# Layer 1's memory queries begin with their first halves, and the first two pairs' values are split in token layout

## The chip, the cores and the metric

The kernel runs on one NeuronCore of one Trainium2 chip, as one launch. The metric is the device time of a launch in microseconds (us), given as the median of several runs. A profile is one execution, recorded by the hardware profiler; its times count from the first instruction of the span.

## The reference

A two-layer decoder trunk on 1024 tokens of width 1024, in float32. Layer 0 mixes a causal multi-scale pooling branch with a cross-attention into 256 memory tokens (4 heads of 128). After it, one projection of the residual stream gives shared keys, values and forget-gate logits. Layer 1 mixes a forgetting attention (16 heads of 64) over these with another memory cross-attention. Cut to what matters here:

```python
def mixer_sublayer(x, mem, w_in, w_mem_kv, w_out, main_fn):
    h = x @ w_in                                  # columns [main | mem q | main gate | mem gate]
    ...
    y_mem = memory_attention(q_mem, mem, w_mem_kv)
    y = jnp.concatenate([y_main * silu(g_main), y_mem * silu(g_mem)], axis=-1)
    return y @ w_out

def memory_attention(q_mem, mem, w_mem_kv):
    mkv = mem @ w_mem_kv                          # keys, values of the 256 memory tokens, 4 heads of 128
    p = softmax(q @ mk.T * 128 ** -0.5)
    return p @ mv

def shared_kv(x, w_kv_shared, b_forget):
    h = x @ w_kv_shared                           # k | v | forget logits
    cum = cumsum(log_sigmoid(f_logit + b_forget), axis=1)

def forgetting_attention(u, k, v, cum):           # causal, 16 heads of 64
    logits = q @ k.T * 0.125 + cum[t] - cum[s]
    return softmax(logits) @ v

x = layer_norm(ALPHA * x + mixer_sublayer(...))   # per layer
```

## The kernel before

Everything is computed with each float32 operand split into a high part (fp32r) and a low part (bf16), three products for one (`three`: high by high, low by high, high by low). `hi_lo` makes the parts: ScalarE casts the high one (line 187), VectorE or GpSimd subtracts for the low one (line 188). A weight slab comes by `split_w`: a DMA into one of four `raw` buffers, then `hi_lo` into one of four `w` and four `wl` buffers. `slab` is one projection of 128 output columns for all 1024 tokens: two weight pieces of 256 KB, then two halves of 512 tokens, 24 products each, every half into one of the two PSUM banks `pj` and evicted from there.

TensorE runs in the order in which the program is written. The other engines and the DMA queue of SyncE run in an order that a scheduler fixes when the kernel is built; each queue is in order, so an instruction that waits holds all behind it.

At the end of layer 0 (`OutProj.rest`, `norm`) the rows of the new residual stream are normed in tiles of 128 tokens, scaled to float16, turned by two DMA transposes each (`turned_rows`) and written to `XH`, `XL`, the transposed operand of all of layer 1's projections. The last two row tiles, 6 and 7, are turned inside `mem_attention` of layer 1 (the list `turns`), before its products.

`mem_attention(1, ...)` then makes four memory keys (`keys(h)`, 24 products of 256 columns each, from `memT`, which `mem_kv` loads and splits), and after that four query slabs `win[1, 8 + h]` with the memory values (`vals(h)`) between them. Its attention over 8 row tiles follows, with gate slabs as filling.

`start_units` makes queries and keys of the first head pair and, through `v_first`, the values of the first two pairs with the forget logits, token by token. `v_turned` turns these values to channel layout with 16 transposes on TensorE and scales and splits them per channel (`values_of`), and four DMA transposes bring them back to token layout. `forget_gates` computes log-sigmoid on VectorE, sums over tokens with one product by a triangle and seven by ones, and writes the sums to DRAM (`cumd`), from which `forget_rows` loads one row per head, broadcast over the partitions (`R`). The sixteen heads of `fox` follow; each softmax needs its `R`.

In the last pair, `OutProj.early` multiplies the first 256 rows of the memory branch's output by its part of the output weights, into four accumulators: two in banks `L`, two in `pj`. The gate slabs just before use `pj` as well.

Of the kernel before, what the change touches and what calls it, by code (L numbers as in the profile page):

```python
# [77 lines left out]
def run(units):  # L78
    for _ in units:
        pass  # L80
# [19 lines left out]
def trunk_kernel(ctx, tc, x, xT, memT, win, wk, wv0, wv, wmk, wmv, wout, poolw, pscale, lng, lnb, bforget, out):  # L100
# [96 lines left out]
        nc.gpsimd.tensor_scalar(hi, src, 1.0, 1.0, ALU.mult, ALU.mult)  # L197
        nc.gpsimd.tensor_tensor(lo[0], src, hi.bitcast(F32), ALU.subtract)  # L198

    def split_w(src_dram, shape, by=nc.vector):  # L200
        r = raw(shape)
        nc.sync.dma_start(r, src_dram)
        h, l = in_place(wt, shape)
        gp_hi_lo(h, l, r) if low[0] else hi_lo(h, l, r, by=by)
        return h, l

# [21 lines left out]
        for i, (a, b) in enumerate(terms):  # L228
            nc.tensor.matmul(acc, a, b, start=i == 0, stop=i == len(terms) - 1)  # L229

    def slab(pieces_dram, XH, XL, evac, banks=("pj", 2)):

        ready = isinstance(pieces_dram, list)
        if ready:
            ws = pieces_dram
        else:
            ws = [split_w(pieces_dram[0], [P, 4, P])]
            yield 0
            ws.append(split_w(pieces_dram[1], [P, 4, P]))
            yield 0  # L240

        def terms(n, kts):
            cols = slice(n * NH, (n + 1) * NH)
            out = []
            for kt in kts:
                h, l = ws[kt // 4]
                out.append(three((h[:, kt % 4, :], cut(l, slice(None), kt % 4)), (XH[:, kt, cols], cut(XL, slice(None), kt, cols))))
            return out

        def put(acc, a, b, start, stop):  # L250
            nc.tensor.matmul(acc, a, b, start=start, stop=stop)  # L251
# [117 lines left out]

    def mem_attention(l, XH, XL, kv, qtile, ytile, yd):  # L370

        (kh, kl, v, undo), keys, vals = kv
        qs = []
        if l:
            while turns:
                turns.pop(0)(lambda: vt([P, D], F16), lambda: vt([P, 2 * KT, P], F16))
            for h in range(4):
                keys(h)
        for h in range(MH):
            qh, ql = in_place(qtile, [P, S])  # L380
# [8 lines left out]
            if not l or h:  # L389
# [62 lines left out]
    class OutProj:  # L452
# [68 lines left out]
        def early(self, y, yh, yl):  # L521


            nc.sync.dma_start(y, self.yd[2, :, :, : 2 * P])
            yield
            for two in (slice(0, 2), slice(2, 4)):
                hi_lo(yh[:, two, :], cut(yl, slice(None), two), y[:, two, :], True)
                yield
            self.accs = self.open(0)
            yield from self.products(self.accs, 2, yh, yl)  # L530

        def rest(self, resid, XH, XL, dst):
            self.split(24)
# [169 lines left out]
    with tc.tile_pool(name="in1", bufs=1) as in1:  # L703
# [7 lines left out]
        def vt(shape, dt=F32R):  # L711
            return sb(shape, "V", 4, dt, in1)

        kv = mem_kv(1)
        with tc.manual_schedule(engines={PE}):
            mem_attention(1, XH, XL, kv, xy, lambda: vt([P, S], F32), y1d[2])
        cumd = dram.tile([HEADS, S], F32, name="cumd")
        fg = G((P, 8, ST * HEADS))
        flog = fg[:, 0, :]
# [18 lines left out]
        unscale, done = const.tile([P, 8], F32, name="unscale"), []  # L738
        toks, first_vs = [], []

        def v_turned():

            for pr in range(2):
                u = MK([P, S], F32)
                for g in range(2):
                    t = ps([P, 4, P], "T", 2)
                    for j in range(4):
                        nc.tensor.transpose(t[:, j, :], toks[g][:, j, pr * P : (pr + 1) * P], ident)
                    nc.scalar.copy(u[:, g * NH : (g + 1) * NH], t.rearrange("p s q -> p (s q)"))
                    yield  # L750
                first_vs.append(values_of(u))

        def v_first():

            wh, wl = zip(*(halved(MK, [P, 4, FW]) for _ in range(2)))
            toks.extend(T([P, 4, 2 * P], F32) for _ in range(2))
            for kt in range(KT):
                r = raw([P, FW])
                nc.sync.dma_start(r, wv0[kt // 2, :, kt % 2, :])
                hi_lo(wh[kt // 4][:, kt % 4, :], cut(wl[kt // 4], slice(None), kt % 4), r)  # L760
            for s in range(ST):
                acc = ps([P, NH], "L", 3)
                terms = []
                for kt in range(KT):
                    at = slice(None), kt, slice(s * P, (s + 1) * P)
                    terms.append(three((XH[at], cut(XL, *at)), (wh[kt // 4][:, kt % 4, :], cut(wl[kt // 4], slice(None), kt % 4))))
                for j, (u, w) in enumerate(grouped(terms, s % 2 == 1)):
                    nc.tensor.matmul(acc[:, :FW], u, w, start=j == 0, stop=j == 3 * KT - 1)
                    yield FW
                nc.scalar.copy(toks[s // 4][:, s % 4, :], acc[:, : 2 * P])  # L770
                nc.vector.tensor_tensor(flog[:, s * HEADS : (s + 1) * HEADS], acc[:, 2 * P : FW], bfb, ALU.add)

        def forget_gates():

            n = ST * HEADS
            a, e, z, q, acc, lf, cum = (fg[:, j, :] for j in range(1, 8))
            lp = a
            nc.vector.tensor_scalar(a, flog, -1.0, None, ALU.mult)
            nc.vector.tensor_tensor(a, a, flog, ALU.max)
            nc.scalar.activation(e, a, AF.Exp, scale=-1.0)  # L780
            nc.vector.tensor_scalar(z, e, 2.0, None, ALU.add)
            nc.vector.reciprocal(z, z)
# [12 lines left out]
            nc.tensor.matmul(ca[:, :n], tri, lf, start=True, stop=False)  # L795
            for d in range(1, ST):
                nc.tensor.matmul(ca[:, d * HEADS : n], ones, lf[:, : n - d * HEADS], start=False, stop=d == ST - 1)
            nc.vector.tensor_copy(cum, ca[:, :n])
            yield
            t = ps([P, 4, P], "T", 2)  # L800
            nc.tensor.transpose(t[:, 0, :], cum, ident)
            rows = tr[:, 0, :]
            nc.vector.tensor_copy(rows, t[:, 0, :])
            for i in range(ST):
                nc.sync.dma_start(cumd[:, i * P : (i + 1) * P], rows[i * HEADS : (i + 1) * HEADS, :])
            yield
# [57 lines left out]
        def start_units(keys, queries, following):  # L864
# [299 lines left out]
```

## Time and profile before

| | |
|---|---|
| median of 3 runs | 1215.21 us (1212.19 to 1216.25) |
| the profiled execution | 1217.81 us, its span 1215.6 us |
| TensorE busy | 1180.0 us, 97% of the span |
| VectorE busy | 798.4 us, 66% |
| ScalarE busy | 616.6 us, 51% |
| GpSimd busy | 200.4 us, 16% |
| granted TensorE clock | 0.996 of full speed |

In rows of the profile, PE is TensorE, DVE is VectorE, ACT is ScalarE, POOL is GpSimd and SPq the DMA queue of SyncE. A timeline row gives start, duration, engine, line, operation, output<-inputs by tile names, count, and in brackets the idle time ahead of it with what ended it. A window row gives for a stretch its length and the busy time of PE, PEld (weight loads), DVE, ACT and POOL, then the granted clock, the DMA engines' share and GB/s. Where rows merge several matmuls, the recorded ends overlap; the pace is read from start to start.

### The profile page before, as it was taken

How to read it: one execution, taken by the hardware profiler on the slowest of the kernel's cores; microseconds unless marked ns; L12 is line 12 of the kernel's file. 1: busy time of each engine (PE TensorE's matmuls, PEld its weight loads, DVE VectorE, ACT ScalarE, POOL GpSimd, SP SyncE). 2: the span in 40 equal slices, each digit the busy share in tenths (PEclk: the TensorE clock that was granted, in tenths of full speed). 3: DMA queues.
4: the chain of work that ended last, by engine and by line, in shares of the span. 5: the costliest groups of instructions: out<-in, count | busy, mean ns of one | idle time of the engine just before them, and what ended most of it. 6: DMA issues, size and time to landing. Idle time of an engine off the chain costs nothing. (4 is left out here: it accounts for less than half of the span.)

```text
span 1215.6 us, 19488 instructions
## 1 busy us (share of the span) xinstructions
PE 1180.0 (97%) x6837; PEld 743.0 (61%) x6954; DVE 798.4 (66%) x1868; ACT 616.6 (51%) x1318; POOL 200.4 (16%) x304
## 2 busy tenths in 40 slices
PE   8999999999999997999999999999999999999997
PEld 4566665555555555666775666666666666655554
DVE  6644767375666657357555878777878878775654
ACT  6433654262522235356333777767766777783110
POOL 2000000000000012100003334333334324530000
PEclk9999999999999999999999999999999999999998
DMA  6333654242445567245527789889897999995431
GB/s 234 108 102 93 133 113 156 78 130 71 142 153 156 156 173 184 77 107 103 175 53 170 158 184 182 177 169 187 176 194 165 196 178 210 235 234 181 167 110 47
DMA packets 284305, 182.83 MB, mean 150 GB/s; under 512 B 229168, under 2 KB 242608, under 8 KB 284208
## 3 DMA queue, kind: packets, MB, share of 16 engines
q1 hardware_dynamic: 284208, 181.59, 61.4%
q8 instruction: 54, 0.88, 0.3%
q14 instruction: 43, 0.35, 0.1%
HBM read 94.97 MB, written 22.61 MB: 97 GB/s over the span
## 5 line engine op out<-in xcount | busy, mean ns | idle before, releaser
L251 PE MATMUL pj<-A,w 128*128 128x512 f32 (+1 forms) x1887 | 600.5, 399 | 3.6 <-ACT A L187 2.2
L251 PE MATMUL pj<-A,wl 128*128 128x512 bf16 x951 | 360.7, 381 | 4.8 <-DVE wl L188 0.6
L251 PEld LDWEIGHTS pj<-A,w 128*128 128x128 f32 x976 | 180.8, 189 | 45.7 <-ACT A L187 3.1
L251 PEld LDWEIGHTS <-w 128*128 128x128 bf16 x992 | 95.8, 98 | 123.3 <-issue 36.0
L251 PEld LDWEIGHTS <-wl 128*128 128x128 bf16 x992 | 97.5, 98 | 95.1 <-issue 5.8
L915 ACT ACTIVATE T<-MK,s 128x512 f32<-128x512 f32 x192 | 111.0, 578 | 58.0 <-DVE s L907 36.7
L937 DVE SCALAR_TENSOR_TENSOR P<-T,s,P 128x512 f16<-128x512 f32 x192 | 111.9, 613 | 31.5 <-ACT P L936 30.0
L936 ACT ACTIVATE P<-T,s 128x512 f16<-128x512 f32 x192 | 102.6, 575 | 48.7 <-issue 27.4
L518 PEld LDWEIGHTS <-T 128*128 128x128 bf16 x736 | 70.6, 98 | 87.3 <-issue 4.4
L188 DVE TENSOR_TENSOR wl<-raw,w 128x512 bf16<-128x512 f32 x98 | 69.2, 712 | 82.8 <-ACT w L187 81.4
L187 ACT CAST w<-raw 128x512 fp32r<-128x512 f32 x106 | 64.8, 617 | 98.5 <-PE pj L251 67.6
L229 PE MATMUL L<-B,B 128*128 128x512 f32 (+3 forms) x384 | 109.9, 389 | 3.2 <-DVE s L907 2.9
L229 PEld LDWEIGHTS L<-B,B 128*128 128x128 f32 x384 | 71.1, 189 | 28.5 <-DVE s L907 9.0
L351 POOL TENSOR_SCALAR A<-A 128x1024 bf16<-128x1024 f32 x8 | 8.4, 1052 | 423.5 <-ACT A L349 423.5
L907 DVE CUSTOM_DVE_ANT_0 MK<-L,R 128x512 f32<-128x512 f32 (+3 forms) x128 | 72.5, 567 | 8.4 <-DMA R<-cumd 5.0
L899 POOL TENSOR_SCALAR_AFFINE_SELECT R<-R 128x128 f32<-128x128 f32 x128 | 41.4, 329 | 207.8 <-DVE s L907 111.5
L198 POOL TENSOR_TENSOR wl<-raw,w 128x512 bf16<-128x512 f32 x54 | 69.1, 1280 | 3.5
L188 DVE TENSOR_TENSOR T<-T,T 128x1024 bf16<-128x1024 f32 x23 | 31.9, 1387 | 50.8 <-ACT T L187 50.7
L187 ACT CAST T<-T 128x1024 fp32r<-128x1024 f32 x23 | 24.1, 1048 | 76.9 <-DMA T<-y1d 50.4
L197 POOL TENSOR_SCALAR w<-raw 128x512 fp32r<-128x512 f32 x54 | 34.3, 634 | 74.8 <-PE pj L251 74.7
L518 PE MATMUL L<-B,T 128*128 128x512 bf16 (+1 forms) x164 | 43.0, 391 | 0.2
L966 PE MATMUL O<-T,V 128*128 128x128 f16 x576 | 38.5, 220 | 4.8 <-DMA T<-P 4.8
(277 smaller groups left out, 1744.1 us busy)
## 6 DMA issues: line engine op xcount, KB each, us to landing
raw<-in_win_dram SPq DMA_DIRECT2D x96, 256.0 KB, 2.9
raw<-in_wout_dram SPq DMA_DIRECT2D x40, 256.0 KB, 2.9
B<-B SPq DMA_DIRECT2D x32, 256.0 KB, 4.9
R<-cumd SPq DMA_DIRECT2D x16, 512.0 KB, 4.5
y0d<-Y SPq DMA_DIRECT2D x12, 512.0 KB, 3.2
T<-y0d SPq DMA_DIRECT2D x12, 512.0 KB, 5.3
T<-y1d SPq DMA_DIRECT2D x11, 512.0 KB, 4.2
raw<-in_wmk_dram SPq DMA_DIRECT2D x16, 256.0 KB, 2.7
```

The costliest lines, as they stand in the source:

```text
L187: pin(nc.scalar.copy(hi, src))
L188: pin(by.tensor_tensor(lo[0], src, hi.bitcast(F32), ALU.subtract))
L198: nc.gpsimd.tensor_tensor(lo[0], src, hi.bitcast(F32), ALU.subtract)
L229: nc.tensor.matmul(acc, a, b, start=i == 0, stop=i == len(terms) - 1)
L251: nc.tensor.matmul(acc, a, b, start=start, stop=stop)
L518: nc.tensor.matmul(acc, y, w, start=c == 2 and j == firsts[id(acc)], stop=c == 1 and j == lasts[id(acc)])
L899: nc.gpsimd.affine_select(R[:, qs], R[:, qs], [[-1, P]], ALU.is_ge, -NEG, base=0, channel_multiplier=1).ins
L907: nc.vector.tensor_tensor_reduce(p[:, lo:up], lg, R[:, lo:up], 1.0, top, ALU.add, ALU.min, m[:, n : n + 1])
L915: nc.scalar.activation(e, p[:, lo:up], AF.Exp, bias=top, scale=-1.0, accum_out=sums[:, n, hd % 2, i : i + 1],)
L936: nc.scalar.activation(pair[:, lo:up], e, AF.Copy, scale=r)
L937: nc.vector.scalar_tensor_tensor(pair[:, L + lo : L + up], e, r, pair[:, lo:up], ALU.mult, ALU.subtract)
L966: nc.tensor.matmul(acc[:, cols(i)], v[:, b, 2 * j : 2 * j + 2, :].rearrange("p e d -> p (e d)"), pt[hd, i][:, j, :], start=n == 0, stop=Fa ...
```

## The change

There are three edits. In layer 1's `mem_attention` the order becomes: weights of all four query slabs, the first two on the `w` and `wl` buffers, the last two on buffers of the pool `P` (`aside_homes`); the turns of row tiles 6 and 7; the first halves (tokens 0 to 511) of all four queries; only then `mem_kv` with its loads of `memT`; then each query's second half with keys and values between and behind. In `start_units`, `v_split` takes the place of `v_turned`: one scale for all values of the first two pairs (a maximum over both tiles, across partitions by one transpose, spread again by one product with ones), and the split straight into token layout, without the 16 transposes and the four DMA transposes. The gates' tile sums are made by six additions on VectorE, so that one product with ones stands where seven stood. And `OutProj.early` multiplies first for the accumulators in `L` and then for those in `pj`.

```diff
-    def slab(pieces_dram, XH, XL, evac, banks=("pj", 2)):
+    def slab(pieces_dram, XH, XL, evac, banks=("pj", 2), make=wt):
...
     def mem_attention(l, XH, XL, kv, qtile, ytile, yd):
 
-        (kh, kl, v, undo), keys, vals = kv
-        qs = []
+        qs = [in_place(qtile, [P, S]) for _ in range(MH)] if l else []
+
+        def query_units(h, make):
+            qh, ql = qs[h]
+            return slab(win[l, 8 + h], XH, XL, lambda cols, acc: hi_lo(qh[:, cols], cut(ql, slice(None), cols), acc), make=make)
+
+        def aside_homes():
+
+            lows = sb([P, 4, 4, P], "P", 4, BF16)
+            for n in range(2):
+                highs = sb([P, 2, 4, P], "P", 4, F32R)
+                left = [[highs[:, k], lows[:, 2 * n + k]] for k in range(2)]
+                yield lambda shape, dt=F32R, left=left: left[0].pop(0) if dt == F32R else left.pop(0)[0]
+
         if l:
+            homes = aside_homes()
+            units = [query_units(h, wt if h < 2 else next(homes)) for h in range(MH)]
+            for two in units:
+                run(islice(two, 2))
             while turns:
                 turns.pop(0)(lambda: vt([P, D], F16), lambda: vt([P, 2 * KT, P], F16))
-            for h in range(4):
-                keys(h)
-        for h in range(MH):
-            qh, ql = in_place(qtile, [P, S])
-            units = slab(win[l, 8 + h], XH, XL, lambda cols, acc: hi_lo(qh[:, cols], cut(ql, slice(None), cols), acc))
-            if l and not h:
-                run(islice(units, 3 * KT + 2))
-                vals(0)
-            run(units)
-            qs.append((qh, ql))
-            if not l:
+            for two in units:
+                run(islice(two, 3 * KT))
+            kv = mem_kv(l)
+        (kh, kl, v, undo), keys, vals = kv
+        for h in range(MH):
+            if l:
+                run(units[h])
+                for what, which in ((), ((keys, 0), (keys, 1)), ((keys, 2), (vals, 0)), ((keys, 3), (vals, 1)))[h]:
+                    what(which)
+            else:
...
+        if l:
+            vals(2)
+            vals(3)
...
-            yield from self.products(self.accs, 2, yh, yl)
+            parts = self.terms(self.accs, 2, yh, yl)
+            yield from self.ordered(grouped(parts[0] + parts[1]) + grouped(parts[2] + parts[3], True), 2)
...
-        def v_turned():
+        def v_split():
+
+            m, e = tiny(2), tiny(1)
+            for g in range(2):
+                nc.vector.tensor_reduce(
+                    m[:, g : g + 1], toks[g].rearrange("p s t -> p (s t)"), AX.X, ALU.max, apply_absolute_value=True,
+                )
+            nc.vector.tensor_tensor(e, m[:, 0:1], m[:, 1:2], ALU.max)
+            yield
+            row, all_ = ps([P, NH], "L", 3), ps([P, NH], "L", 3)
+            nc.tensor.transpose(row[:1, :P], e, ident)
...
+            nc.tensor.matmul(all_[:, :1], ones[:1, :], top[:1], start=True, stop=True)
...
+                for b in range(2):
+                    u, (hi, lo) = toks[pr][:, :, 64 * b : 64 * b + 64], (v[:, b, e::2, :] for e in range(2))
+                    nc.scalar.activation(hi, u, AF.Copy, scale=sc)
+                    nc.vector.scalar_tensor_tensor(lo, u, sc, hi, ALU.mult, ALU.subtract)
...
+            nc.vector.tensor_copy(q[:, :HEADS], lf[:, :HEADS])
+            for d in range(1, ST - 1):
+                own, before = (slice((d - k) * HEADS, (d - k + 1) * HEADS) for k in range(2))
+                nc.vector.tensor_tensor(q[:, own], q[:, before], lf[:, own], ALU.add)
+
             yield
             ca = ps([P, 2 * P], "O", 1)
             nc.tensor.matmul(ca[:, :n], tri, lf, start=True, stop=False)
-            for d in range(1, ST):
-                nc.tensor.matmul(ca[:, d * HEADS : n], ones, lf[:, : n - d * HEADS], start=False, stop=d == ST - 1)
+            nc.tensor.matmul(ca[:, HEADS:n], ones, q[:, : n - HEADS], start=False, stop=True)
...
             gates = forget_gates()
             next(gates)
-            for _ in v_turned():
-                yield from islice(own, 6)
-            yield from islice(own, 33)
+            split = v_split()
+            yield from islice(own, 45)
+            next(split)
+            yield from islice(own, 31)
             next(gates)
             yield from islice(own, 7)
             next(gates)
+            for n in (8, 14):
+                yield from islice(own, n)
+                next(split)
             yield from own
```

ScalarE's queue at the seam of the layers, before. `raw..` are loaded pieces, `w..` query or key weights, `MK..<-pj..` evictions of memory keys; `V663` and `V666` are the scaled rows of tiles 6 and 7, `A500<-V..` their way into `XH`.

```order
L344 ACTIVATE V663_4081<-G636_3998,unrow_3145 128x1024
L187 CAST w685_4184<-raw684_4182 128x512
L580 ACTIVATE s647_4029<-s646_4028 128x1
L187 CAST MK658_4074<-pj669_4101 128x256
L187 CAST w688_4190<-raw687_4188 128x512
L194 CAST MK659_4075<-MK658_4074 128x256
L349 ACTIVATE A500_3059<-V665_4085,unrow_3145 128x8x128
```

The same place after the change. `T687` and `T689` are the two halves of `memT`, `P660` the fourth query's weights, `B650<-pj683` and `B652<-pj684` the evictions of the first halves of queries 0 and 1; `V677` and `V680` are row tiles 6 and 7.

```order
L344 ACTIVATE V677_4103<-G636_3998,unrow_3145 128x1024
L187 CAST T687_4231<-raw691_4235 128x512
L194 CAST T688_4232<-T687_4231 128x512
L187 CAST T687_4231<-raw692_4240 128x512
L194 CAST T688_4232<-T687_4231 128x512
L349 ACTIVATE A500_3059<-V679_4107,unrow_3145 128x8x128
L600 ACTIVATE s647_4029<-s646_4028 128x1
L187 CAST P660_4062<-raw675_4095 128x512
L187 CAST P660_4062<-raw676_4099 128x512
L187 CAST B650_4052<-pj683_4123 128x512
L187 CAST T689_4233<-raw693_4245 128x512
L187 CAST T689_4233<-raw694_4250 128x512
```

The rows right behind these:

```order
L194 CAST T690_4234<-T689_4233 128x512 x2
L344 ACTIVATE V680_4113<-G643_4020,unrow_3145 128x1024
L187 CAST B652_4054<-pj684_4150 128x512
L349 ACTIVATE A500_3059<-V682_4117,unrow_3145 128x8x128
L187 CAST B654_4056<-pj685_4177 128x512
```

What moved: the casts of `memT`, which stood ahead of row tile 6, now stand around it, and the query evictions stand among the turns of tiles 6 and 7, each behind a load.

SyncE's queue at the seam, before. `raw..` are the four buffers in turn, `x1` the store of row tile 6, `V665` that tile's turned rows.

```order
L289 DMA raw656_4064<-in_memT_dram 128x512
L289 DMA raw657_4069<-in_memT_dram 128x512
L202 DMA raw670_4102<-in_wmk_dram 128x512
L202 DMA raw673_4108<-in_wmk_dram 128x512
L202 DMA raw677_4142<-in_wmk_dram 128x512
L202 DMA raw680_4148<-in_wmk_dram 128x512
L202 DMA raw684_4182<-in_wmk_dram 128x512
L589 DMA x1_177<-G636_3998 128x1024
L202 DMA raw687_4188<-in_wmk_dram 128x512
L202 DMA raw691_4222<-in_wmk_dram 128x512
L202 DMA raw694_4228<-in_wmk_dram 128x512
L347 DMA_TRANSPOSE V665_4085<-V663_4081 128x8x128
```

The same place after the change; `V679` is the turned tile 6.

```order
L202 DMA raw673_4087<-in_win_dram 128x512
L202 DMA raw674_4091<-in_win_dram 128x512
L609 DMA x1_177<-G636_3998 128x1024
L202 DMA raw675_4095<-in_win_dram 128x512
L202 DMA raw676_4099<-in_win_dram 128x512
L289 DMA raw691_4235<-in_memT_dram 128x512
L289 DMA raw692_4240<-in_memT_dram 128x512
L347 DMA_TRANSPOSE V679_4107<-V677_4103 128x8x128
L348 DMA_TRANSPOSE V679_4107<-V678_4104 128x8x128
L289 DMA raw693_4245<-in_memT_dram 128x512
L289 DMA raw694_4250<-in_memT_dram 128x512
```

What moved: the query weights have the buffers first, and the two halves of `memT` stand on both sides of tile 6's transposes.

The DMA queue of SyncE between the gates and the first head, before. `cumd` are the gates' sums, `R` the rows of the first two heads, `V..<-MK..` the values' DMA transposes, `raw1030`, `raw1049` and `raw1052` weight loads.

```order
L735 DMA_TRANSPOSE V954_5943<-MK950_5931 128x16x64 x2
L822 DMA B914_5574<-B913_5573 64x1024 x2
L822 DMA B916_5576<-B915_5575 64x1024 x2
L735 DMA_TRANSPOSE V962_5991<-MK958_5979 128x16x64 x2
L202 DMA raw1030_6311<-in_win_dram 128x512
L805 DMA cumd_5551<-G906_5553 16x128 x8
L202 DMA raw1049_6382<-in_win_dram 128x512
L202 DMA raw1052_6392<-in_win_dram 128x512
L884 DMA R981_6153<-cumd_5551 128x1024
```

After the change:

```order
L865 DMA B909_5569<-B908_5568 64x1024 x2
L865 DMA B911_5571<-B910_5570 64x1024 x2
L202 DMA raw1017_6286<-in_win_dram 128x512
L202 DMA raw1036_6357<-in_win_dram 128x512
L202 DMA raw1039_6367<-in_win_dram 128x512
L848 DMA cumd_5546<-G901_5548 16x128 x8
L931 DMA R968_6128<-cumd_5546 128x1024
```

What moved: the four transposes are gone, and two weight loads stand ahead of the sums that stood behind them.

More of the change, by code (lines that the diff above doesn't have):

```diff
@@ L236, in slab @@
         else:
-            ws = [split_w(pieces_dram[0], [P, 4, P])]
+            ws = [split_w(pieces_dram[0], [P, 4, P], make=make)]
             yield 0
-            ws.append(split_w(pieces_dram[1], [P, 4, P]))
+            ws.append(split_w(pieces_dram[1], [P, 4, P], make=make))
             yield 0
@@ L712, in vt @@
             return sb(shape, "V", 4, dt, in1)
-        kv = mem_kv(1)
         with tc.manual_schedule(engines={PE}):
-            mem_attention(1, XH, XL, kv, xy, lambda: vt([P, S], F32), y1d[2])
+            mem_attention(1, XH, XL, None, xy, lambda: vt([P, S], F32), y1d[2])
         cumd = dram.tile([HEADS, S], F32, name="cumd")
@@ L739, in trunk_kernel @@
         toks, first_vs = [], []
-        def v_turned():
-            for pr in range(2):
[L744 to L751, printed above, removed]
+        def v_split():
[8 more added lines that the diff above has]
+            nc.tensor.transpose(row[:1, :P], e, ident)
+            top = tiny(1)
+            nc.vector.tensor_reduce(top[:1], row[:1, :P], AX.X, ALU.max)
+            nc.vector.tensor_scalar(top[:1], top[:1], 2.0 ** -100, None, ALU.max)
+            nc.vector.tensor_scalar(top[:1].bitcast(I32), top[:1].bitcast(I32), 0x7F800000, None, ALU.bitwise_and)
+            yield
+            nc.tensor.matmul(all_[:, :1], ones[:1, :], top[:1], start=True, stop=True)
+            un, sc = unscale[:, :1], tiny(1)
+            nc.vector.tensor_scalar(un, all_[:, :1], 2.0 ** -15 / PSCALE, None, ALU.mult)
+            nc.vector.reciprocal(sc, all_[:, :1])
+            nc.vector.tensor_scalar(sc, sc, 2.0 ** 14, None, ALU.mult)
+            for pr in range(2):
+                done.append(0)
+                v = vt([P, 2, 2 * ST, 64], F16)
+                for b in range(2):
+                    u, (hi, lo) = toks[pr][:, :, 64 * b : 64 * b + 64], (v[:, b, e::2, :] for e in range(2))
+                    nc.scalar.activation(hi, u, AF.Copy, scale=sc)
+                    nc.vector.scalar_tensor_tensor(lo, u, sc, hi, ALU.mult, ALU.subtract)
+                first_vs.append((v, un))
+            yield
@@ L753, in v_first @@
         def v_first():
             wh, wl = zip(*(halved(MK, [P, 4, FW]) for _ in range(2)))
-            toks.extend(T([P, 4, 2 * P], F32) for _ in range(2))
+            toks.extend(T([P, ST, P], F32) for _ in range(2))
             for kt in range(KT):
@@ L769, in v_first @@
                     yield FW
-                nc.scalar.copy(toks[s // 4][:, s % 4, :], acc[:, : 2 * P])
+                for pr in range(2):
+                    nc.scalar.copy(toks[pr][:, s, :], acc[:, pr * P : (pr + 1) * P])
                 nc.vector.tensor_tensor(flog[:, s * HEADS : (s + 1) * HEADS], acc[:, 2 * P : FW], bfb, ALU.add)
```

7 lines of the change are left out of this document (4 added, 3 removed).

## The prediction

> **What bounds the kernel now.** I read the page first, then the busy time by stretches, then TensorE's waits in the stretches that the edits touch, then the timelines of the engines that it waits for there.
>
> ```profile
> span 1215.6 us, 19488 instructions
> PE 1180.0 (97%) x6837; PEld 743.0 (61%) x6954; DVE 798.4 (66%) x1868; ACT 616.6 (51%) x1318; POOL 200.4 (16%) x304
> 456.00:482.80 26.80, 20.60 (x147) 15.36 (x147) 20.33 (x32) 15.18 (x29) 8.94 (x6) 1.00 0.79 193
> PE pj L229 <- DVE T L188: 2.8, 1, 2.8
> ```
>
> TensorE bounds the kernel: 97% busy, 35.6 us idle in all. So only two things can pay: products that go away, and waits that go away and don't come back. The second stretch of interest is the seam of the layers, 456.0 to 482.8, where TensorE idles 26.80 - 20.60 = 6.2 us, 2.8 of it for the low part of `memT`. That is the largest pool of idle time that this change touches.
>
> **Edit 1, the seam.** The products only change places: four first halves of queries first, keys and values behind. What counts is the waits.
>
> ```profile
> 456.35 0.27 PE L229 MATMUL pj<-T,w 128*128 128x256 bf16 x1
> 460.14 0.27 PE L229 MATMUL pj<-T,w 128*128 128x256 bf16 x1 [2.75 <-DVE T L188]
> 473.68 1.19 PE L251 MATMUL pj<-A,w 128*128 128x512 f32 x4
> 475.43 0.39 PE L251 MATMUL pj<-A,wl 128*128 128x512 bf16 x1 [0.56 <-DVE wl L188]
> 479.61 0.29 PE L229 MATMUL pj<-T,w 128*128 128x256 bf16 x1
> ```
>
> Layer 0's last product ends at 456.35. Query 0's first half took from 473.68 to 479.61 with 0.56 us of waiting, so a half takes 5.4 us, and four of them cover 456.35 to 477.8. The first halves read tokens 0 to 511 only, turned long before. But the halves share the two `pj` banks: query 2 can't start before query 0 is evicted, at 456.35 + 10.7 = 467.1, nor query 3 before query 1 is. And the evictions now stand in ScalarE's queue among the turns of row tiles 6 and 7. So I follow that queue.
>
> ```profile
> 445.76 0.60 PE L518 MATMUL L<-W,T 128*128 128x512 bf16 x2
> 453.86 1.27 DVE L586 SCALAR_TENSOR_TENSOR G<-G,s,P 128x1024 f32<-128x1024 f32 x1
> 457.13 0.68 DVE L575 SCALAR_TENSOR_TENSOR G<-G,L 128x512 f32<-128x512 f32 x1
> 457.73 1.17 DVE L188 TENSOR_TENSOR wl<-raw,w 128x512 bf16<-128x512 f32 x1
> 461.27 1.24 SPq L347 DMA_TRANSPOSE V<-V  x1
> 467.44 1.15 ACT L349 ACTIVATE A<-V,unrow 128x1024 fp32r<-128x1024 f16 x1 [1.46 <-DMA V<-V]
> 473.21 1.25 SPq L347 DMA_TRANSPOSE V<-V  x1
> 477.23 1.15 ACT L349 ACTIVATE A<-V,unrow 128x1024 fp32r<-128x1024 f16 x1 [0.90 <-DMA V<-V]
> 480.19 0.58 ACT L187 CAST B<-pj 128x512 fp32r<-128x512 f32 x1
> 450.80 0.62 ACT L187 CAST w<-raw 128x512 fp32r<-128x512 f32 x1 [1.53 <-DMA raw<-in_wmk_dram]
> 458.07 1.13 ACT L194 CAST T<-T 128x512 bf16<-128x512 f32 x2
> DMA to landing us min/median/max: 2.9/3.9/4.8
> ```
>
> The last row is that of the `memT` loads (line 289). VectorE can begin tile 6's norm when its products are done, at 446.1 (those for tile 7 start at 445.76). Up to the low part of query 2's weights, whose `raw` buffers `memT`'s first half then takes, stand twelve operations 512 wide at 0.6 us (457.13 to 457.73), two 1024 wide at 1.2 and about 1.2 us of small ones: 10.8, so 456.9. Only behind these two loads does SyncE issue tile 6's transposes, at about 457.4. From issue to the cast that uses them took 6.2 us (461.27 to 467.44) and 4.0 (473.21 to 477.23), so the cast starts at 461.4 to 463.6. On ScalarE follow in order that cast 1.15, a square root 0.2, two weight casts and the eviction of query 0 at about 0.6 each, 3.1 us; then VectorE's half of the eviction, 0.7 us and some queueing. Query 0's bank is free at 466.9 to 467.9, and is wanted at 467.1: a wait of up to 0.9, I take 0.7.
>
> The second half of `memT` can't be loaded before query 3's weights are out of their buffers, about 466.6. It lands 2.9 to 4.8 later, at the median at 470.5. Behind it on ScalarE stand its cast 0.6, two copies 1.13, tile 7's scaling 1.15 and query 1's eviction 0.58, to 473.9; VectorE then does tile 7's other half and the low part, to about 475.4. Query 3 wants the bank at 467.1 + 0.7 + 5.4 = 473.2: a wait of 2.2, with bounds 1.0 to 3.6 from the landing and the start. Query 0's second half starts at about 480.8; tile 7's cast, 4.0 us behind its transposes at 473.4, ends by 478.6, so that step hides. The weights of later keys and values reuse `w` buffers of queries that are a whole half (5.4 us) past; their cast and subtraction, under 3 us, hide behind it.
>
> So waits of 3.0 us (1.0 to 4.5) take the place of 6.2: **3.2 us gained** (1.7 to 5.2).
>
> [...]
>
> **Edit 2, values and gates.** I measure from V = 621.09, the end of `v_first`.
>
> ```profile
> 621.09 0.60 PE L748 MATMUL T<-ident,T 128*128 128x128 f32 x4
> 624.71 0.60 PE L748 MATMUL T<-ident,T 128*128 128x128 f32 x4
> 625.15 0.38 PE L251 MATMUL pj<-A,w 128*128 128x512 bf16 x1
> 635.74 0.38 PE L795 MATMUL O<-G,G 128*128 128x128 f32 x2
> 637.45 0.38 PE L251 MATMUL pj<-A,wl 128*128 128x512 bf16 x1
> 651.23 1.28 PE L229 MATMUL L<-B,B 128*128 128x512 f32 x4
> 653.53 0.81 PE L229 MATMUL L<-B,B 128*128 128x512 f32 x2
> 654.67 0.62 PE L229 MATMUL L<-B,B 128*128 128x384 f32 x2 [0.33 <-DVE s L907]
> 642.43 4.52 SPq L805 DMA_DIRECT2D cumd<-G  x8
> 648.50 0.80 SPq L884 DMA_DIRECT2D R<-cumd  x2
> 653.92 0.69 DVE L907 CUSTOM_DVE_ANT_0 MK<-L,R 128x512 f32<-128x512 f32 x1 [4.97 <-DMA R<-cumd]
> 640.93 0.62 POOL L197 TENSOR_SCALAR w<-raw 128x512 fp32r<-128x512 f32 x1
> 641.63 1.27 POOL L198 TENSOR_TENSOR wl<-raw,w 128x512 bf16<-128x512 f32 x1
> ```
>
> Four transposes take 0.44 us (624.71 to 625.15), sixteen 1.76. The eight gate products take 1.71 (635.74 to 637.45); two of them about 0.45. A transpose and a tiny product come in, 0.2. TensorE saves 1.76 + 1.26 - 0.2 = 2.8 us. The six additions and two maxima lie on VectorE, which must end the gates by the 76th product; it loses the per-channel scaling in that stretch and has 19 products more until then, which is the cover. Without it `R` would come later by what is left of them.
>
> But the first softmax waits for `R`. Without transposes and gate products the 118 products from V to the first head take 30.14 - 1.76 - 1.71 - 0.1 = 26.6, 0.225 each. Before, the sums stood behind 57 products and 16 transposes; now they stand behind 76 products, 17.1 us after V, so 2.5 later. From there to the DMA queue it takes product 0.45, copy, seven products, transpose and copy, to V + 19.9 or so. Before, the first `cumd` write went at V + 21.3, held by the values' DMA transposes, which are gone. From that write to the softmax's first use took 653.92 - 642.43 = 11.5, so now V + 31.4 instead of V + 32.8: 1.4 earlier. TensorE reaches the point of its wait (654.67 before) 2.8 earlier, and waits there 1.4 us longer. **1.4 us gained**; bounds 0.5 (a slower `R`) and 2.8 (a faster one).
>
> Who waits for the new order of loads: `raw1036` and `raw1039` stand ahead of `cumd` and need GpSimd's splits of two query-side weights, whose buffers the first pair's queries leave at the 62nd and 70th product, V + 14.0 and V + 15.8. With 0.62 for a cast and 1.27 for a subtraction GpSimd ends them at V + 16.4 and V + 18.4: 1.5 us of slack.
>
> **Edit 3, the accumulators' order.**
>
> ```profile
> 1080.65 0.74 PE L518 MATMUL pj<-V,B 128*128 128x512 f32 x2 [1.47 <-DVE G L282]
> 1088.41 0.47 PE L972 MATMUL O<-T,V 128*64 128x128 f16 x10
> 1096.68 0.68 ACT L978 ACTIVATE G<-O,unscale 64x512 f32<-64x512 f32 x1
> 1110.73 1.04 ACT L187 CAST T<-T 128x1024 fp32r<-128x1024 f32 x1 [9.10 <-DMA T<-y1d]
> 1111.82 0.73 PE L518 MATMUL L<-R,T 128*128 128x512 f32 x2 [0.84 <-ACT T L187]
> ```
>
> The `pj` products stand 20 products later, over 4 us, and the 1.47 us wait for the last gate's bank goes. But at 1111.82 TensorE waits for the last heads' output, which came by an eviction at 1096.68 that had its input since 1088.88 and stood in ScalarE's queue behind weight casts; from there to the load's cast at 1110.73 nothing asks TensorE. That chain isn't moved, so the 0.84 becomes 2.3: **0 gained** (0 to 1.5).
>
> **The sum.** 3.2 + 1.4 + 0 = 4.6 us, from 1217.8 of the profiled execution to 1213.2. That execution lies 2.6 above the median of the runs shown, so I take the difference off the median: 1215.2 - 4.6 = 1210.6. A measurement of this kernel tells about 0.3%, 3.6 us, from no change. The waits of the sixteen heads I leave as they are: everything there is counted from the arrival of `R`.
>
> **Rivals.**
>
> *The wait changes its name.* ScalarE's queue holds the evictions so long that the seam still costs 6.2 us. For it: nearly every step of ScalarE there ends on a DMA. Against it: it needs 3.2 us more than my chain, over its upper end. 1.4 gained: 1213.8 on the median.
>
> *Neither arrival binds.* `memT` lands in 2.9 us, and `R` comes as early as TensorE. Against it: 11.5 us of DMA chain before. 5.2 + 2.8 = 8.0 gained: 1207.2.
>
> [...]
>
> *Slower: SyncE's queue holds the sums.* If the two loads ahead of `cumd` wait for buffers that the second pair's keys leave at the 118th product, not the queries at the 70th, `R` comes 48 x 0.225 = 10.8 less 1.5 of slack, 9.3 us later, and TensorE stands. 4.6 - 9.3 = 4.7 slower: 1219.9. It decides once GpSimd's second split ends later than V + 20; beyond that each us costs one. Against it: four `w` buffers go round, and the queries' come up first.
>
> **How the numbers follow.** My forecast 0.50, the renamed wait 0.20, neither arrival binding 0.15, the gap 0.05, slower 0.10. Within the forecast the lower bounds add to 2.2, and the upper ends run into the second rival; I put three quarters of it over 3.6. Faster by over 0.3%: 0.37 + 0.15 = 0.52. Within: 0.13 + 0.20 + 0.05 = 0.38. Slower: 0.10. The range reaches from the second rival, 1207.0, over the first and third to no gain, 1215.5, and leaves out the slower case and little more.
>
> **What would show it.** After the change: no `memT` wait of a key at the seam; two waits of line 251 for the low parts of query evictions, the second the longer, the idle sum about 3.0. From `v_first`'s last product to the first head about 27.4 us, and there a wait of about 1.7 us (0.33 before) for line 907's successor, which itself waits for `R`. No wait in the early products, and over 2 us at the one for the last heads' output. I am wrong if the seam's idle time stays near 6, if `cumd` is written later after V than before, or if the early wait's end moves the kernel's end.

## The result and the profile after

The changed kernel takes 1208.74 us (median of 6 runs, 1207.27 to 1209.80), the kernel before on the same chip 1214.15 (6 runs, 1212.19 to 1216.25): ratio 0.9957, 95% interval 0.9943 to 0.9971. That is 5.4 us faster where 4.6 were forecast. The sum came out by luck: two of its terms were wrong, one too low and one too high, as the stages show.

The page of the changed kernel, its span and engines:

```profile
span 1207.7 us, 19444 instructions
PE 1176.2 (97%) x6813; PEld 740.8 (61%) x6929; DVE 802.3 (66%) x1874; ACT 615.1 (51%) x1324; POOL 200.7 (17%) x304
```

TensorE's longest waits in it (us in total, times, longest); those for line 187's `A` lie at the kernel's start:

```profile
PE L L229 <- DVE s L954: 4.9, 8, 2.4
PE O L1013 <- DMA T<-P: 4.2, 5, 1.5
PE L L537 <- ACT T L187: 1.9, 1, 1.9
...
PE pj L251 <- ACT A L187: 1.2, 2, 0.8
PE O L840 <- DVE G L835: 1.0, 1, 1.0
```

No line of the seam is left among them. New are the 2.4 us for the first softmax (line 954, formerly 907; 0.33 before), the 1.0 for the gates' sums (line 835), and the 1.9 for the last heads' output (0.84 before).

The stretches, busy times as in the prediction, granted clock third from the end. The first is the seam:

```profile
455.16:481.98 26.82, 26.71 (x121) 15.16 (x122) 14.94 (x26) 12.41 (x21) 3.35 (x3) 1.00 0.61 146
1100.00:1103.00 3.00, 1.14 (x6) 0.61 (x4) 0.72 (x1) 1.04 (x1) 0.00 (x0) 1.00 0.93 312
1103.00:1107.00 4.00, 4.00 (x13) 3.14 (x12) 2.61 (x3) 2.70 (x3) 0.00 (x0) 0.57 0.21 74
1107.00:1112.00 5.00, 4.95 (x24) 2.34 (x24) 2.86 (x4) 0.68 (x1) 0.00 (x0) 1.00 0.00 0
```

The seam's idle time is 0.1 us (6.2 before). Behind the wait for the last heads the clock stands at half for 3.4 us, which no term of the sum held.

TensorE's timeline at the landmarks of the prediction:

```profile
455.16 1.51 PE L251 MATMUL pj<-A,w 128*128 128x512 f32 x5
612.32 1.98 PE L251 MATMUL pj<-A,w 128*128 128x512 f32 x8
630.53 0.47 PE L840 MATMUL O<-G,G 128*128 128x112 f32 x2 [0.99 <-DVE G L835]
640.97 1.28 PE L229 MATMUL L<-B,B 128*128 128x512 f32 x4
646.52 0.61 PE L229 MATMUL L<-B,B 128*128 128x384 f32 x2 [2.44 <-DVE s L954]
1102.30 0.74 PE L537 MATMUL L<-R,T 128*128 128x512 f32 x2 [1.86 <-ACT T L187]
```

Each row answers to one of before: 456.35, 621.09 (V), 651.23 (the first head), 654.67 and 1111.82. The differences give the 7.9 us between the two spans (1215.6 and 1207.7): 1.2 ahead of the seam, where nothing was edited; **7.6** from the seam to V (164.74 to 157.16); **0.6 lost** from V to the end of the first softmax wait (33.58 to 34.20); 1.4 gained from there to the end of the last heads' wait (the 1.47 us wait gone, 1.0 of it back at the later one, the rest shorter waits in the heads); **1.6 lost** behind it.

### The profile page after: what moved, and what is told of

The parts are those of the page before. It is cut to its first block, busy times and chain, and to the rows that moved or that the text cites. A ratio compares the mean times of both kernels' runs of the same rounds, so it can differ in the third digit from the quotient of the medians.

```text
span 1207.7 us, 19444 instructions
## 1 busy us (share of the span) xinstructions
PE 1176.2 (97%) x6813; PEld 740.8 (61%) x6929; DVE 802.3 (66%) x1874; ACT 615.1 (51%) x1324; POOL 200.7 (17%) x304
## 5 line engine op out<-in xcount | busy, mean ns | idle before, releaser
L251 PE MATMUL pj<-A,w 128*128 128x512 bf16 (+1 forms) x1825 | 580.2, 398 | 3.1 <-ACT A L187 1.2
L251 PE MATMUL pj<-A,wl 128*128 128x512 bf16 x921 | 348.4, 379 | 4.5 <-issue 0.5
L251 PEld LDWEIGHTS pj<-A,w 128*128 128x128 f32 x944 | 174.8, 188 | 43.7 <-ACT A L187 2.4
L251 PEld LDWEIGHTS <-w 128*128 128x128 bf16 x960 | 92.7, 98 | 119.4 <-issue 35.0
L251 PEld LDWEIGHTS <-wl 128*128 128x128 bf16 x960 | 94.2, 98 | 91.3 <-issue 6.1
```

## The experiments

All were timed against the kernel before in the same runs of a chip. The table gives the ratio with its interval and three stretches from each trace, between the start times of the rows above: the seam to V, V to the end of the last heads' wait, and from there to the end.

```
kernel              ratio   interval         seam-V   V-last   last-end
before              1                        164.74   490.73   103.78
changed             0.9957  0.9943-0.9971    157.16   489.98   105.40
e1_seam             0.9948  0.9935-0.9960    157.16   489.41   103.96
e2_gates            1.0007  0.9998-1.0015    162.04   491.57   103.83
e3_early            0.9998  0.9986-1.0011    164.65   490.97   105.46
e4_no_early         0.9960  0.9946-0.9974    157.30   489.72   103.79
e5_split_late       0.9930  0.9917-0.9942    157.16   488.74   103.85
e6_mask_first       0.9918  0.9905-0.9931    157.16   484.98   103.96
e7_both             0.9941  0.9928-0.9955    157.16   487.51   103.82
e8_both_no_early    0.9930  0.9917-0.9942    157.14   487.65   103.81
e9_gates_later      0.9916  0.9902-0.9929    157.16   486.11   103.87
e10_sums_on_tensor  0.9935  0.9918-0.9952    157.16   486.83   104.94
e11_mask_no_early   0.9917  0.9904-0.9929    157.16   486.59   103.98
e12_evict_first     0.9960  0.9946-0.9973    157.16   492.16   103.93
```

A trace is one execution, the ratio is of all. The profiled execution of e3_early lies 4.0 us above its kernel's median, those of e4_no_early and e6_mask_first 2.6 and 1.7 us below theirs, so a stretch that differs by 1 or 2 us between two kernels need not show in their ratios.

### One edit at a time

**e1_seam**, the first edit alone on the kernel before:

```diff
+            for two in units:
+                run(islice(two, 2))
...
+            for two in units:
+                run(islice(two, 3 * KT))
+            kv = mem_kv(l)
```

> The kernel before with the first edit alone: queries' first halves ahead of keys and values at the seam. The prediction's sum: waits of about 3.0 us stay at the seam, so 3.2 us faster than before. Theory from the two traces (every wait of the seam goes, and with each wait some 0.16 us of refilling that its row does not count): the stretch from layer 0's last product to the end of the forget gates' products is 7.6 us shorter, no idle time in it, so about 7.5 us faster, 1206.7 against 1214.2. Rival (the waits come back where the two layers' other stages meet): under 4 us.

Measured: 0.9948, 6.3 us faster, no less than the whole change. The interval reaches from 4.9 to 7.9 us: the prediction's 3.2 is excluded, the theory's 7.5 is not. The seam stretch is 157.16, as in the changed kernel. The old seam took 162.0 in the trace of e2_gates and 164.7 in those of before and e3_early (the last holds about 3 us of half clock, by the pace of its products), so the gain depends on which execution of before one takes.

**e2_gates**, the second edit alone:

```diff
-            for _ in v_turned():
-                yield from islice(own, 6)
-            yield from islice(own, 33)
+            split = v_split()
+            yield from islice(own, 45)
+            next(split)
+            yield from islice(own, 31)
```

> The kernel before with the second edit alone: V of the first two pairs scaled and split by tokens, gates' sums on VectorE. The prediction: 1.4 us faster (TensorE saves 2.8, 1.4 of it waits for R). Theory from the two traces: the mask on R stands behind four weight operations of GpSimd and the softmax behind V's split on VectorE, so from the end of the forget gates' products to the end of TensorE's first wait for the softmax it takes 34.2 us instead of 33.6: 0.6 slower, at most 1.0 faster by fewer waits in the heads. Rival: V's work taken off ScalarE and SyncE frees the first heads, and the kernel is over 2 us faster.

Measured: 1.0007, 0.9 us slower, but the interval reaches no change, so a loss is not shown. The prediction's 1.4 faster is excluded (it would be 0.9988). TensorE's timeline, and the stretch behind the wait:

```profile
651.78 1.01 PE L229 MATMUL L<-B,B 128*128 128x384 f32 x2 [2.43 <-DVE s L935]
```

```profile
651.70:655.10 3.40, 3.32 (x8) 1.43 (x9) 2.89 (x10) 1.60 (x4) 0.58 (x2) 0.51 0.80 164
```

The same wait as in the changed kernel, and here the half clock follows it.

**e3_early**, the third edit alone:

```diff
-            yield from self.products(self.accs, 2, yh, yl)
+            parts = self.terms(self.accs, 2, yh, yl)
+            yield from self.ordered(grouped(parts[0] + parts[1]) + grouped(parts[2] + parts[3], True), 2)
```

> The kernel before with the third edit alone: the early accumulators' order. The prediction: the 1.47 us wait goes and the wait for the last heads' output grows by as much: 0. Theory from the two traces: the longer wait (near 2.3 us) also brings the granted clock to half for some 3.3 us, which costs 1.6: 0 to 1.7 us slower. Rival: the eviction of the last heads starts earlier too, and 1.5 us are gained.

**e4_no_early**, the changed kernel without it (the same lines the other way round):

> The changed kernel without the third edit. The prediction: as the changed kernel, 1208.7, within 0.5 us. Theory that the longer wait costs the clock: the two short waits (1.5 and 0.8) are back, the granted clock stays 1.00 between 1095 and 1125 us, and the kernel is 1.0 to 1.8 us faster than the changed one, about 1207.3. Rival: the low clock there was this one profiled execution's alone: no difference in the times, and a low clock may show in any of these runs.

Measured: 0.9998 alone, and 0.9960 against 0.9957 without it: nothing either way. TensorE's timeline of e3_early, and its clock:

```profile
1111.14 0.74 PE L518 MATMUL L<-R,T 128*128 128x512 f32 x2 [2.35 <-ACT T L187]
```

```profile
1112.40:1115.90 3.50, 3.50 (x10) 2.70 (x9) 2.10 (x3) 2.75 (x3) 0.00 (x0) 0.52 0.11 39
```

The wait of 0.84 became 2.35, the prediction's 2.3. From V to the end of that wait it takes 490.97 us against 490.73: the 1.47 is swallowed whole. Then the clock halves and the tail is 1.7 longer. That theory's price does not show in the medians, so it is not paid in every execution (1.6 in each would be 1.0013); e4's trace, with waits of 1.3 and 0.2, has its products at full pace there (0.45 us a pair, against 0.85 in e3's half clock), as its theory said, but its times are no better than the changed kernel's.

### What stands ahead of the first softmax

The changed kernel's timelines of VectorE and GpSimd:

```profile
627.40 3.08 DVE L835 TENSOR_TENSOR G<-G 128x16 f32<-128x16 f32 x4
639.57 5.45 DVE L787 SCALAR_TENSOR_TENSOR V<-T,s,V 128x512 f16<-128x512 f32 x4 [0.84 <-ACT V L786]
645.77 0.69 DVE L954 CUSTOM_DVE_ANT_0 MK<-L,R 128x512 f32<-128x512 f32 x1
640.17 1.60 POOL L198 TENSOR_TENSOR wl<-raw,w 128x512 bf16<-128x512 f32 x1
642.88 1.59 POOL L198 TENSOR_TENSOR wl<-raw,w 128x512 bf16<-128x512 f32 x1
644.43 0.74 POOL L946 TENSOR_SCALAR_AFFINE_SELECT R<-R 128x128 f32<-128x128 f32 x1
```

Before, nothing but the key evictions stood ahead of the first softmax on VectorE, and GpSimd's mask on `R` came ahead of the second gate's weights. Now V's four low parts and four weight operations stand there. Two experiments take one queue each out of the way.

**e5_split_late**: V's low parts behind the second row tile's softmax.

```diff
-                    nc.vector.scalar_tensor_tensor(lo, u, sc, hi, ALU.mult, ALU.subtract)
+                    with tc.issue_after(softmaxed[-1]):
+                        nc.vector.scalar_tensor_tensor(lo, u, sc, hi, ALU.mult, ALU.subtract)
```

> The changed kernel with VectorE's four low parts of V queued behind the second row tile's softmax of the first head instead of ahead of the first. In the changed kernel TensorE waited 2.4 us there; VectorE's low parts ended at 645.0 us and GpSimd's mask on R, behind two weight splits, at 645.2. Theory that the two engines slow each other (low parts 1.4 us each, splits 1.3 to 1.6 instead of 1.27): with VectorE out of the way GpSimd's splits end near 643.3, the mask near 643.6, and the wait falls from 2.4 to 0.5 or less: some 2 us faster than the changed kernel, near 1206.7. Rival, that GpSimd's queue alone binds at 645.2: the first softmax starts 0.6 earlier and no more. Rival, that R itself lands late: no gain at all.

**e6_mask_first**: GpSimd's second gate split behind the first mask.

```diff
+        low.append(0)
+        with tc.issue_after(first_mask[0]) if len(low) in (4, 5) else nullcontext():
...
+            first_mask.append(masked[-1])
```

> The changed kernel with the second gate's two weight splits on GpSimd queued behind the first mask on R. Theory that the two engines slow each other: VectorE's low parts, 1.4 us each beside the splits, run in 0.7 to 1.0, end near 643, and TensorE's wait falls from 2.4 to 1 or less. Rival, that each queue binds by itself: VectorE still ends at 645.0 and the wait stays at 2.4. Rival, that R lands late: no gain, with the mask itself waiting for the load.

Measured: 0.9930 and 0.9918. GpSimd in e5_split_late, and VectorE's first softmax:

```profile
639.55 1.28 POOL L198 TENSOR_TENSOR wl<-raw,w 128x512 bf16<-128x512 f32 x1
642.76 0.29 POOL L950 TENSOR_SCALAR_AFFINE_SELECT R<-R 128x128 f32<-128x128 f32 x1
642.12 0.69 DVE L959 CUSTOM_DVE_ANT_0 MK<-L,R 128x512 f32<-128x512 f32 x1
```

VectorE and GpSimd in e6_mask_first:

```profile
639.01 2.74 DVE L791 SCALAR_TENSOR_TENSOR V<-T,s,V 128x512 f16<-128x512 f32 x4 [0.84 <-ACT V L790]
642.50 0.69 DVE L959 CUSTOM_DVE_ANT_0 MK<-L,R 128x512 f32<-128x512 f32 x1
641.20 0.71 POOL L950 TENSOR_SCALAR_AFFINE_SELECT R<-R 128x128 f32<-128x128 f32 x1 [11.31 <-DMA R<-cumd]
```

With GpSimd's splits out of the way the four low parts take 2.74 us, not 5.45; with VectorE's low parts out of the way the subtraction takes 1.28, not 1.60. In both TensorE's wait of 2.4 is gone. In these traces the two engines slow each other, and the doubling of the low parts, 2.7 us, is enough for the wait of 2.4. The rival that GpSimd's queue binds falls: in e5_split_late the first softmax starts at 642.12, ahead of the mask at 642.76, for it reads the first 512 columns and the mask concerns the last 128. The rival of a late `R` falls with the last row: it landed at 641.2, 29.4 us after V (611.76). By the ratios e6_mask_first is 4.7 us faster than the changed kernel. The wait and its refilling make 2.6 of that. The wait for the last heads and the half clock behind it, 1.9 and 1.6 in the changed kernel's trace, are absent in this one; how often they come is not known.

**e7_both**, both moves, and **e8_both_no_early**, both without the third edit (their diffs are those above):

> Both moves in the changed kernel. R's load, issued at 637.8, takes 3.8 to 4.7 us, so the mask could start at 641.6 to 642.5 and the softmax 0.3 later, before TensorE wants its bank at 644.1: the wait falls from 2.4 to 0.5 or less, and the second edit is then worth near the 1.4 to 2 us that the prediction gave it: near 1206.5. Rival, that the work only moves into the next row tiles: the first wait falls and others of the first head grow by as much, no gain.

> Both moves, and the early accumulators in their former order. Theory that waits near 2 us and over now and then bring half clock for 3.3 us, at 1.6 us each: no wait of over 1.6 us is left in this kernel after the start, the granted clock stays 1.00, and it is the fastest of all, 1.5 to 3 us under the changed kernel, with the narrowest spread of times. Rival: as the kernel with both moves, within 0.5.

Measured: 0.9941 and 0.9930; neither is better than e6_mask_first alone (0.9918, whose interval overlaps both). The wait of 2.4 is gone in both, but V's low parts, 0.75 us each, now lie between the softmaxes of the first rows, and from V to the last heads it takes 2.5 and 2.7 us more than in the trace of e6_mask_first, up to 1.7 of which may belong to that one execution. This points to the rival: moved on VectorE, the work comes back in the next row tiles; beside a silent GpSimd, it can stay where it was. e8 was not the fastest, so clearing the long waits was not enough.

### The smaller terms, on e6_mask_first

**e9_gates_later**: `islice(own, 36)` ahead of the sums.

```diff
-            yield from islice(own, 31)
+            yield from islice(own, 36)
...
-            for n in (8, 14):
+            for n in (8, 9):
```

> The kernel with the mask ahead of the second gate's splits, with the gates' sums on TensorE five products later (after 81 instead of 76). VectorE's six additions for them ended 1.0 us after TensorE wanted them, four of them beside GpSimd's subtractions at 0.77 us each against 0.19 for the two ahead. Theory: they end where they did, five products are 1.08 us, so the wait of 1.0 goes, with some 0.16 of refilling, and R is no later: 1.1 us faster if TensorE has that much slack at the first softmax, else down to 0.3. Near 1203.2 (against 1204.05). Rival: R leaves later by as much and the first head waits for it, no gain.

**e10_sums_on_tensor**: the gates' sums as eight products again.

```diff
-            nc.tensor.matmul(ca[:, HEADS:n], ones, q[:, : n - HEADS], start=False, stop=True)
+            for d in range(1, ST):
+                nc.tensor.matmul(ca[:, d * HEADS : n], ones, lf[:, : n - d * HEADS], start=False, stop=d == ST - 1)
```

> The kernel with the mask ahead of the second gate's splits, with the gates' sums over tiles on TensorE again (eight products, no additions on VectorE). The prediction had this part of the second edit save 1.26 us of TensorE's time; in the changed kernel the additions brought a wait of 1.0 us and some 0.16 of refilling. Theory: the two cancel, the same time within 0.3 us, no wait at the sums and eight products of 1.7 us there. Rival: the sums on VectorE save 1.2 net of the wait, and this kernel is slower by that.

**e11_mask_no_early**: e6_mask_first without the third edit.

> The kernel with the mask ahead of the second gate's splits, with the early accumulators in their former order. In that kernel the wait for the last heads' output showed none, so the third edit isn't swallowed there: theory, the wait of 1.2 to 1.5 us for the gate's bank comes back and nothing pays for it, 1.3 us slower, near 1205.4. Rival: the chain of the last heads is as long as before and only ran early by chance: the same time within 0.5 us.

Measured: 0.9916, 0.9935, 0.9917. In e9 the wait at the sums is gone and 0.41 us comes back at the transpose behind them; V to the first head falls from 28.64 to 28.21 us, 0.4 of the 1.1 expected at best, and the times don't tell it from e6. In e10 that stretch is 28.64, with eight products and no wait: the sums on VectorE save TensorE nothing, as the theory said. Why its time is 2 us worse (the intervals overlap) stays open; in its trace 1.0 us of that lies behind the last heads' wait (104.94 against e6's 103.96). e11 has the 1.47 wait for the bank again, and from V to the last heads 1.6 more than e6, but the same time, as the rival had it. The wait for the last heads differs from trace to trace (none in e6 and e11, 0.4 to 2.0 in e5, e7, e9 and e10). From ScalarE's eviction to its cast of what is loaded back took 12.0 us in e6 and 14.1 in e5; what sets that is not shown.

**e12_evict_first**: on e9, the output weights from the eighth slot on cast behind the last heads' eviction.

```diff
-            self.split(24)
+            self.split(14)
+            with tc.issue_after(evicted[0]) if evicted else nullcontext():
+                self.split(24)
```

> The kernel with the mask first and the gates' sums five products later, with the ten output-weight halves from the eighth slot on cast by ScalarE behind the last heads' eviction instead of ahead of it. There the eviction had its input at 1075.6 us, ran at 1085.8, and TensorE waited 1.6 us for the cast of what was loaded back. Theory that this queue sets that wait: the eviction runs near 1076, the load's cast some 8 us earlier than its need, the wait of 1.6 goes and with it now and then 1.6 us of half clock; 1.5 to 2 us faster than that kernel, near 1202.8, and the third edit is then a gain of its own. Rival: the weight loads behind the store in SyncE's queue come 2 us later and a wait for weights takes the place, no gain. Rival: other loads set the wait, it stays at 1.6.

Measured: 0.9960 against e9's 0.9916, some 5.3 us worse. ScalarE's timeline, and TensorE's:

```profile
1079.73 1.04 ACT L187 CAST T<-T 128x1024 fp32r<-128x1024 f32 x1 [5.96 <-DMA T<-y1d]
1080.80 0.68 ACT L1034 ACTIVATE G<-O,unscale 64x512 f32<-64x512 f32 x1
1081.51 1.14 ACT L187 CAST MK<-raw 128x512 fp32r<-128x512 f32 x2
```

```profile
1083.74 2.15 PE L543 MATMUL L<-MK,T 128*128 128x512 bf16 x4 [5.12 <-DVE MK L188]
```

A miss: the eviction, whose input was there at 1074.9, stood behind a cast that waited 6 us for its load, and the weights stood behind both. The wait for the last heads did go, as the queue theory wanted, but a wait for weights of 5.1 took its place, and the granted clock was 0.83 on the mean from 1080 to 1100 us, as 6.8 us of half clock make it. The best version run is e6_mask_first (e9 and e11 are as good): 1204.05 us, 10 us under the kernel before.

## Why the prediction was right, and where not

- **Seam: right in kind, half the size** (3.2 forecast, 6.3 timed in e1). The `memT` wait went and the halves cover. But the two waits of 3.0 us for evictions that were to stay never came. The step that failed is "the second half of `memT` can't be loaded before query 3's weights are out of their buffers": it took the buffers of `memT`'s first half. The rows below are of the changed kernel, SyncE, ScalarE and VectorE:

```profile
459.29 1.50 SPq L289 DMA_DIRECT2D raw<-in_memT_dram  x2
462.89 0.58 ACT L187 CAST B<-pj 128x512 fp32r<-128x512 f32 x1
467.52 0.57 ACT L187 CAST B<-pj 128x512 fp32r<-128x512 f32 x1
464.43 0.68 DVE L188 TENSOR_TENSOR B<-pj,B 128x512 bf16<-128x512 f32 x1
468.85 0.68 DVE L188 TENSOR_TENSOR B<-pj,B 128x512 bf16<-128x512 f32 x1
```

  Those loads go 4.1 us after the seam's start, not 10.2. Query 0's bank is free at 465.1, wanted at 466.0; query 1's at 469.5, wanted at about 471.4 (a half takes 5.4). For query 0 the prediction's own steps were also added too high: from a cast at 461.4 they give 465.2 (461.4 + 3.1 + 0.7), not 466.9. Most of the rest of the miss is that an idle row undercounts a wait: a 256-column product is booked with 0.27 us while the next starts 0.11 behind it, so each wait costs its row plus 0.16. Seven waits make 1.1 of the 7.6.
- **Values and gates: the gain did not come** (1.4 forecast; e2's interval leaves at most 0.2 us of it, and the traces lose 0.6). TensorE's saving was nearly there: V to the first head 28.65 (27.4 forecast, 30.14 before), the 1.2 between them the wait for the sums and its refilling. VectorE, "which must end the gates by the 76th product", missed that by 1.0 us: four of the six additions took 3.08 us, beside GpSimd's splits. The first `cumd` write went at V + 20.7 (19.9 forecast), and in e6, where the mask shows it, `R` landed at V + 29.4 (the first write at V + 20.7 there too), 8.7 us later: the chain of `R` was shorter than thought. The step that failed is "From that write to the softmax's first use took 653.92 - 642.43 = 11.5": it took `R` for the only thing ahead of the softmax. V's split had been moved in front of it on VectorE, next to GpSimd's splits, and the softmax came at V + 33.5 instead of 31.4. The prediction did not follow the queues of those two engines there.
- **Early order: right**, 1.47 swallowed, 0.84 turned into 1.9 to 2.4.
- **The rivals.** The chance of 0.05 for "the gap", the third rival of the range (1214.1), stood on a wait of 3.6 us at the seam that lowers the clock. No run shows such a wait or a half clock in the new seam: the changed kernel's granted clock is 1.00 there (455.16 to 481.98). Its half clock came behind the last heads' wait of 1.86 us. The loads ahead of `cumd` did no harm: its first write was 0.8 later than forecast, not 9. "Neither arrival binds" was true of the seam.
- So 4.6 came near 5.4 by luck: 3.2 was too little by about 3 (e1: 6.3 timed), and 1.4 too much by about 2 (e2: -0.9).

## What to carry to other kernels

When work moves between engines, list what newly stands ahead of each critical instruction in every queue, and what the neighbouring engine does meanwhile: an operation's price is that of its row only beside the same neighbours (V's four low parts: 5.45 us beside GpSimd's splits, 2.74 without). Removing a wait pays more than its row (0.16 us more at the seam), putting it elsewhere pays nothing (e3), and a queue order that is free on the mean can cost a lot behind one load (e12). Time each edit alone before crediting the sum.

## What the runs showed of the hardware

- **VectorE and GpSimd slowed each other.** Low parts of V took 1.06 to 1.77 us each beside GpSimd's splits, 5.45 for four (changed), and 2.74 for four without (e6); a subtraction on GpSimd 1.60 beside them, 1.28 without (e5). The 16-wide additions took 0.17 to 1.13 in the changed kernel; no run takes GpSimd away from them.
- **The clock halved behind some gaps of about 2 us, and not behind others.** It did after 1.86 (changed), 2.43 (e2) and 2.35 us (e3), each time for 3.4 us at a cost of 1.6 to 1.7; it did not right after 2.75 and 2.27 (seam, before and e3), 2.44 and 2.43 (first head, changed and e4), 1.98 (e5). In e3's seam it halved 12 us behind that 2.27, where the gaps were only 0.29 to 0.91: from 470.9 us on a 256-column product took 0.21 us instead of 0.11, for about 3 us. Around the 5.12 us of e12 the granted clock was 0.83 over 20 us. What decides between these is not shown.
- **A stretch without waits repeats to 0.02 us**: seam to V 157.14 to 157.16 in ten of eleven traces that have the new seam, while the old one took 162.0 to 164.7 in three.
